# Ragged self-attention on one core: loops over pairs of ranks with doubled buffers, x transposed by the DMA crossbar, scores in batches of two

## The chip, the cores and the metric

The kernel runs on one core of a Trainium2 chip. TensorE (PE) multiplies, VectorE (DVE) and ScalarE (ACT) read its results out of PSUM, GpSimd (POOL) works from SBUF to SBUF, and SyncE (SP) issues DMAs on the core's 16 DMA engines. The metric is the device time of one execution in microseconds; less is better.

## The reference

Thirty-two sequences of up to 512 rows by 512 columns, each with its own length (75 to 502 in this draw; 64 to 511 by the rule), go through one projection and eight heads of softmax attention. Rows past the length are zero in the output.

```python
for b in range(batch):
    seq_len = lengths[b]
    qkv = np.matmul(x[b, :seq_len], w_qkv)
    q, k, v = np.split(qkv, 3, axis=-1)        # then 8 heads of 64 each
    ...
    scores = scale * np.matmul(q, k.transpose(0, 2, 1))
    attn = np.exp(scores - max)
    attn = attn / (np.sum(attn, axis=-1, keepdims=True) + 1e-08)
    output[b, :seq_len] = np.matmul(attn, v).transpose(1, 0, 2).reshape(seq_len, dim)
```

## The kernel before

**Ranks and classes.** The lengths are known only on the chip. DVE and one small PE matmul sort them, longest first; `idx` holds the order, `masks` the valid rows of each rank, and `ends` how many ranks are at least as long as each of 15 classes N = 512, 480, ... 64. Every engine loads the 15 ends into registers (`load_ends`) and walks the same While loops, one for each class (`loops`), with one rank as an iteration. T = ceil(N / 128) is the number of row tiles: in this draw 4 ranks have T = 4, 12 have T = 3, 11 have T = 2 and 5 have T = 1, and twelve classes are used; 480 and 416, between used ones, have no ranks and are jumped over.

**The pipeline.** The body of rank r computes the attention of rank r, and between its parts the projections of rank r + 1, so that PE has matmuls while ACT takes exponentials. The strings in `make_body` write out the order: S is one unit of scores (both heads of a head pair, one tile of keys) into one of two slots `psc`, evacuated by ACT's exponential into `ep` (L237); Q, K and V are projections into one of two banks `pa`, evacuated by DVE (L266, L299); A is the product with V into `pav`; M and X are the normalization of A on DVE: reciprocal (L357), mask (L364), multiplication into `onat` (L376). `v_aug` has a column of ones (mask values) for each head, so that A yields the softmax sum too.

**Buffers.** There is one `xT`, one `qkT`, one `v_aug`. At a body's end PE transposes the next rank's x16 through the banks `pa` (L397), ACT and DVE copy the results into `xT` (L402, L405), and the next body begins. Its first A takes both score slots free first (`acquire` of s0 and s1), and thus waits for the exponentials of the S just ahead of it.

**Other queues.** SP zero-fills rows past T tiles, loads x three ranks ahead when POOL has cast the one before (s_xfree), and stores the output in four pieces, one for a head pair (s_of, s_od). POOL casts x from float32 to float16. A PE wait shows in the profile as PEq at L35, the helper `take`; matmuls recorded as L424 are the first of a body.

Of the kernel before, what the change touches and what calls it, by code (L numbers as in the profile page):

```python
# [7 lines left out]
FP32 = mybir.dt.float32  # L8
F16 = mybir.dt.float16
I32 = mybir.dt.int32  # L10
# [7 lines left out]
NR = 36  # L18
# [3 lines left out]
class Prog:  # L22


    def __init__(self, busy):
        self.ops = {"pe": [], "act": [], "dve": []}
        self.busy = dict(busy)

# [44 lines left out]
def kernel(  # L73
# [25 lines left out]
    x_p = [sb("x_p0", [P, NT, D], FP32), sb("x_p1", [P, NT, D], FP32)]  # L99
# [8 lines left out]
    ident_f = sb("ident_f", [P, P], FP32)  # L108
    ident = sb("ident", [P, P], F16)
    len_b = sb("len_b", [P, 2 * B], I32)  # L110
    len_c = sb("len_c", [B, 2], I32)
    lenf = sb("lenf", [P, B], FP32)
# [6 lines left out]
    pos_i = sb("pos_i", [B, B], I32)  # L119
    pos_f = sb("pos_f", [B, B], FP32)  # L120
    rk_i = sb("rk_i", [B, NR], I32)
    rk_f = sb("rk_f", [B, NR], FP32)
    bi_i = sb("bi_i", [B, P], I32)
    bi_f = sb("bi_f", [B, P], FP32)
    thr_i = sb("thr_i", [1, len(CLASSES), B], I32)
    thr_f = sb("thr_f", [1, len(CLASSES), B], FP32)
# [5 lines left out]
    row_i = sb("row_i", [P, NT], I32)  # L132
    row_f = sb("row_f", [P, NT], FP32)
    masks = sb("masks", [P, NR - 2, 2, NT], FP32)
    rcp = sb("rcp", [P, NPAIR, 2 * NPAIR], FP32)
    junk = sb("junk", [P, 2], FP32)
# [4 lines left out]
    pa16 = pa.bitcast(F16)  # L141
# [4 lines left out]
    s_xp = [sem("s_xp0"), sem("s_xp1")]  # L146
    s_x = sem("s_x")
    s_const = sem("s_const")
    s_iota = sem("s_iota")
    s_r = sem("s_r")  # L150
    s_m = sem("s_m")
    s_self = sem("s_self")
    s_pself = sem("s_pself")
    s_hot = sem("s_hot")
    s_srt = sem("s_srt")
    s_tab = sem("s_tab")
    s_zero = sem("s_zero")
# [14 lines left out]
    free = {b: sem(f"e_{b}") for b in banks}  # L172

# [671 lines left out]
```

## Time and profile before

| | us |
|---|---|
| median of three runs | 527.71 (522.52 to 530.04) |
| the profiled execution | 529.94 |
| its span, first to last instruction | 528.1 |
| PE busy | 409.9 (78%) |
| PE's weight loads | 275.7 (52%) |
| DVE busy | 284.1 (54%) |
| ACT busy | 243.8 (46%) |
| POOL busy | 58.9 (11%) |
| mean granted PE clock | 0.94 |

A busy share is an average over some 58 us ahead of the loops, in which PE does little, and 32 bodies that get shorter and shorter. Weight loads overlap matmuls. The body's windows and the places where two bodies meet say more than the page's totals.

### The profile page before, as it was taken

How to read it: one execution, taken by the hardware profiler on the slowest of the kernel's cores; microseconds unless marked ns; L12 is line 12 of the kernel's file. 1: busy time of each engine (PE TensorE's matmuls, PEld its weight loads, DVE VectorE, ACT ScalarE, POOL GpSimd, SP SyncE). 2: the span in 40 equal slices, each digit the busy share in tenths (PEclk: the TensorE clock that was granted, in tenths of full speed). 3: DMA queues.
4: the chain of work that ended last, by engine and by line, in shares of the span. 5: the costliest groups of instructions: out<-in, count | busy, mean ns of one | idle time of the engine just before them, and what ended most of it. 6: DMA issues, size and time to landing. Idle time of an engine off the chain costs nothing. (4 is left out here: it accounts for less than half of the span.)

```text
span 528.1 us, 15112 instructions
## 1 busy us (share of the span) xinstructions
PE 409.9 (78%) x5090; PEld 275.7 (52%) x5090; DVE 284.1 (54%) x725; ACT 243.8 (46%) x299; POOL 58.9 (11%) x81
## 2 busy tenths in 40 slices
PE   0008895989895998898888988899888868886973
PEld 0013553555462555565555655665566656675752
DVE  8504552555452654565556555564465654665673
ACT  2003573767572664555556545454343343334331
POOL 9021101010101001101110011101000010001000
PEclk9999997999897998999999989998798898989899
DMA  4080221332313133233323333333333344544575
GB/s 161 1 318 0 80 60 35 113 92 85 123 40 103 50 120 126 68 103 124 124 70 109 124 114 106 101 104 124 119 122 122 128 137 141 166 154 139 169 247 204
DMA packets 60596, 61.07 MB, mean 116 GB/s; under 512 B 3088, under 2 KB 40976, under 8 KB 60560
## 3 DMA queue, kind: packets, MB, share of 16 engines
q1 hardware_dynamic: 59984, 58.50, 34.0%
q10 hardware_dynamic: 576, 2.10, 1.1%
q8 instruction: 21, 0.34, 0.3%
q14 instruction: 15, 0.12, 0.1%
HBM read 27.03 MB, written 33.55 MB: 115 GB/s over the span
## 5 line engine op out<-in xcount | busy, mean ns | idle before, releaser
L237 ACT ACTIVATE ep<-psc 128x896 f16<-128x896 f32 (+5 forms) x262 | 212.2, 810 | 189.5 <-ACTq L35 187.4
L197 PE MATMUL pa<-xT,w_r 128*128 128x352 f16 (+11 forms) x1050 | 168.5, 300 | 0.8 <-PEq L35 0.6
L266 DVE CAST qkT<-pa 128x352 f16<-128x352 f32 (+5 forms) x190 | 106.0, 558 | 88.4 <-DVEq L35 86.2
L197 PEld LDWEIGHTS pa<-xT,w_r 128*128 128x128 f16 x1050 | 83.0, 102 | 54.1 <-issue 29.8
L197 PE MATMUL pav<-v_aug,ep 128*128 128x65 f16 x1768 | 78.3, 199 | 38.0 <-PEq L35 37.8
L197 PE MATMUL pa<-w_r,xT 128*128 128x128 f16 (+1 forms) x1268 | 97.0, 227 | 0.1
L197 PEld LDWEIGHTS pav<-v_aug,ep 128*128 128x128 f16 x1768 | 67.4, 101 | 53.1 <-issue 50.4
L197 PE MATMUL psc<-qkT 64*128 64x352 f16 (+11 forms) x621 | 91.5, 311 | 1.5 <-PEq L35 1.5
L718 POOL CAST x<-x_nat 128x1536 f16<-128x1536 f32 (+3 forms) x32 | 39.8, 1242 | 436.1 <-POOLq L717 436.1
L197 PEld LDWEIGHTS pa<-w_r,xT 128*128 128x128 f16 x1268 | 80.1, 101 | 10.5 <-issue 5.3
L357 DVE RECIPROCAL rcp<-pav 128x6 f32<-128x6 f32 (+2 forms) x113 | 21.5, 190 | 94.4 <-DVEq L35 94.3
L402 ACT COPY xT<-pa 128x1024 f16<-128x1024 f16 (+2 forms) x34 | 29.7, 874 | 82.0 <-ACTq L35 82.0
L299 DVE TENSOR_TENSOR v_aug<-pa,masks 128x384 f16<-128x384 f32 (+2 forms) x112 | 59.4, 531 | 14.8 <-DVEq L35 13.0
L376 DVE TENSOR_TENSOR onat<-pav,rcp 128x384 f32<-128x384 f32 (+2 forms) x113 | 59.3, 525 | 7.3 <-DVEq L35 0.7
L397 PE MATMUL pa<-ident,x 128*128 128x128 f16 x348 | 28.4, 222 | 31.2 <-PEq L35 30.1
L197 PEld LDWEIGHTS psc<-qkT 64*128 64x128 f16 x621 | 26.8, 94 | 44.1 <-issue 32.3
L397 PEld LDWEIGHTS pa<-ident,x 128*128 128x128 f16 x348 | 21.2, 99 | 39.0 <-issue 39.0
L364 DVE TENSOR_SCALAR rcp<-rcp,masks 128x2 f32<-128x2 f32 (+1 forms) x113 | 25.2, 223 | 1.4 <-DVEq L35 1.0
L405 DVE COPY xT<-pa 128x768 f16<-128x768 f16 (+1 forms) x18 | 10.8, 602 | 24.5 <-DVEq L35 24.5
L424 PE MATMUL psc<-qkT 64*128 64x352 f16 (+9 forms) x27 | 8.0, 297 | 17.1 <-PEq L35 16.8
L727 PE MATMUL pav<-onehot,sel 32*128 32x36 f16 x2 | 0.2, 198 | 18.7 <-DVEq L69 18.7
L424 PEld LDWEIGHTS psc<-qkT 64*128 64x128 f16 x27 | 2.5, 93 | 20.9 <-issue 20.8
(50 smaller groups left out, 55.8 us busy)
## 6 DMA issues: line engine op xcount, KB each, us to landing
x_nat<-in_x_dram SPq DMA_DIRECT2D x12, 768.0 KB, 4.5
out_dram<-onat SPq DMA_DIRECT2D x48, 192.0 KB, 2.1
out_dram<-zt SPq DMA_DIRECT2D x11, 512.0 KB, 3.0
x_nat<-in_x_dram SPq DMA_DIRECT2D x11, 512.0 KB, 3.6
out_dram<-onat SPq DMA_DIRECT2D x44, 128.0 KB, 1.8
out_dram<-onat SPq DMA_DIRECT2D x21, 256.0 KB, 2.3
x_nat<-in_x_dram SPq DMA_DIRECT2D x5, 1024.0 KB, 5.4
out_dram<-zt SPq DMA_DIRECT2D x5, 768.0 KB, 3.7
```

The source lines that it names most:

```text
L197: return lambda e: e.matmul(o, lhsT, rhs, start=start, stop=stop)
L237: lambda e: e.activation(out=dst, in_=src, func=AF.Exp, scale=scale),
L266: group(pr, b, eng, mms, lambda e: e.tensor_copy(out=dst, in_=src))
L299: lambda e: e.tensor_tensor(out=v_aug[:, 0:T, 2 * i : 2 * i + 2, 0:HD], in0=pa[:, bank, 0 : T * P].rearrange("p (t a d) -> p t a d", a=2, ...
L357: lambda e: e.reciprocal(out=rv, in_=res[:, :, :, HD]).then_inc(s_r, 1),
L364: lambda e: e.tensor_scalar(out=last, in0=last, scalar1=3.0e38, scalar2=now[0][:, 1, T - 1 : T], op0=ALU.min, op1=ALU.mult,).then_inc(s_m, 1),
L376: lambda e: e.tensor_tensor(out=dst, in0=res[:, :, :, 0:HD], in1=rv.unsqueeze(3).broadcast_to([P, nq, 2, HD]), op=ALU.mult,).then_inc(s_of ...
L397: mms.append(lambda e, o=o, i_=i_: e.transpose(o, i_, ident))
L402: lambda e, d=dst, s=src: e.copy(out=d, in_=s))
L405: lambda e, d=dst, s=src: e.tensor_copy(out=d, in_=s))
L424: ins = f(*a, **k)
L718: e.tensor_copy(out=x16[:, 0:T, :], in_=x_nat[:, 0:T, :]).then_inc(s_x16, 1)
```

## The change

**Pairs.** A loop's iteration now holds two ranks, two halves h = 0 and 1, in the class of the first and longer one. `x_nat`, `x16`, `xT`, `qkT`, `v_aug` and `onat` exist twice, one for each half; half h computes the attention from buffers h and projects the next rank into buffers g = 1 - h. `ends` counts pairs.

**The crossbar.** SP issues one DMA transpose for each tile of 128 rows from `x16[h]` to `xT[h]` (`to_xT`), for the rank two ahead, at the start of half h when PE's first matmul there has said that `xT[h]` is free (s_xtf). PE waits for all of them (s_xt, 64) ahead of a half's first projection. PE's transposes, their copies on ACT and DVE and the identity matrix are gone.

**Batches.** `ORDER` writes S two at a time, and pair 0's scores of the next rank are the last of a half, not mixed with its own start. An A takes a score slot only if the slot last held scores of that head pair.

**Normalization.** For T = 2 and 3 two head pairs' A lie side by side in `pav`, and one reciprocal, mask and multiplication serve both. The output is stored in two pieces of 256 columns, not four of 128.

**POOL, SP and the start.** POOL also writes the ones of `v_aug`. x is loaded five ranks ahead. Ahead of the loops the iotas are written in float32, several DVE casts are gone, the V weights' cast goes from POOL to ACT, the memset of `ep` from POOL to DVE (with a new one of `qkT[1]`), and `load_ends` waits for s_end, after the sort, where `ends` used to be ready ahead of it.

On PE the names are the tiles: `psc` scores, `pa` projections (`xT,w_r` for Q and K, `w_r,xT` for V; `ident,x` transposes), `pav` products with V. Before, the end of the class of N = 384 and the start of N = 352:

```order
L397 MATMUL pa<-ident,x 128x128 x12
L584 REGISTER_ALU
L582 UNCONDITIONAL_BRANCH
L582 ISA
L582 COMPARE_AND_BRANCH
L424 MATMUL psc<-qkT 128x352
L197 MATMUL psc<-qkT 128x352
L197 MATMUL pav<-v_aug,ep 128x65 x18
L197 MATMUL psc<-qkT 128x352 x2
L197 MATMUL pa<-xT,w_r 128x352 x4
L197 MATMUL psc<-qkT 128x352 x2
```

PE at the same place now:

```order
L194 MATMUL pa<-xT,w_r 128x384 x4
L194 MATMUL pa<-w_r,xT 128x128 x12
L539 REGISTER_ALU
L537 UNCONDITIONAL_BRANCH
L537 ISA
L537 COMPARE_AND_BRANCH
L194 MATMUL psc<-qkT 128x352 x4
L194 MATMUL pa<-xT,w_r 128x352 x4
L194 MATMUL pav<-v_aug,ep 128x65 x18
L194 MATMUL pa<-xT,w_r 128x352 x4
L194 MATMUL psc<-qkT 128x352 x4
L194 MATMUL pa<-w_r,xT 128x128 x12
```

The twelve transposes are gone, scores stand four matmuls (two units) together, and a projection lies between them and the first product with V.

On SP one body of N = 352 before (`zt` is the zero fill, TENSOR_LOAD reads the rank's batch index):

```order
L631 DMA out_dram<-zt 128x512
L605 ISA
L606 TENSOR_LOAD idx
L607 ISA
L611 DMA x_nat<-in_x_dram 128x3x512
L605 ISA
L606 TENSOR_LOAD idx
L657 ISA
L657 DMA out_dram<-onat 128x3x128
L657 ISA
L657 DMA out_dram<-onat 128x3x128
```

SP in the first half of N = 352 now:

```order
L574 DMA_TRANSPOSE xT<-x_0 128x4x128 x2
L574 DMA_TRANSPOSE xT<-x_0 128x4x96
L546 ISA
L547 TENSOR_LOAD idx
L548 ISA
L610 DMA out_dram<-zt 128x512
L623 REGISTER_ALU
L623 DMA out_dram<-onat 128x3x256
L546 ISA
L547 TENSOR_LOAD idx
L548 ISA
L582 DMA x_nat<-in_x_dram 128x3x512
```

Three transposes stand ahead of the half's zero fill on the one queue, and the load comes behind the first output.

The diff, cut to its core:

```diff
-    x_nat = sb("x_nat", [P, NT, D], FP32)
-    x16 = sb("x16", [P, NT, D], F16)
-    xT = sb("xT", [P, NC, MAXS], F16)
-    qkT = sb("qkT", [P, 2 * NPAIR, MAXS], F16)
-    v_aug = sb("v_aug", [P, NT, NH, HD + 1], F16)
+    x_nat = [sb(f"x_nat_{h}", [P, NT, D], FP32) for h in range(2)]
+    x16 = [sb(f"x16_{h}", [P, NT, D], F16) for h in range(2)]
+    xT = [sb(f"xT_{h}", [P, NC, MAXS], F16) for h in range(2)]
+    qkT = [sb(f"qkT_{h}", [P, 2 * NPAIR, MAXS], F16) for h in range(2)]
+    v_aug = [sb(f"v_aug_{h}", [P, NT, NH, HD + 1], F16) for h in range(2)]
     ep = sb("ep", [P, NPAIR, 2, NT, MAXS], F16)
-    onat = sb("onat", [P, NT, D], FP32)
+    onat = [sb(f"onat_{h}", [P, 2, NT, 2 * P], FP32) for h in range(2)]
...
+        for b in ("s0", "s1"):
+            if pr.pair[b] == i or T == 1 and pr.pair[b] is not None:
+                acquire(pr, b)
...
+            jobs = [(256 * qt, i, qt) for qt in range(T)]
+        else:
+            jobs = [(74 * (4 * qt + 2 * (i % 2)), i, qt) for qt in range(T)]
...
+        if T in (2, 3) and i % 2 == 0:
+            acquire_carry(pr, mms)
+            return
...
-    def transposes(pr, T, engs, bank=0):
-        n = 2 if T >= 3 else 1
-        w = T * P
-        pr.take("pe", s_x16)
...
+    ORDER = {
+        4: "S S Q0 A0 S S K0 V0 S S Q1 A1 S S K1 V1 S S Q2 A2 S S K2 V2 S S Q3 A3 S S K3 V3",
+        3: "S S Q0 A0 K0 S S V0 Q1 A1 S S K1 V1 S S Q2 A2 K2 S S V2 Q3 A3 S S K3 V3",
+        2: "S S B0 w A0 V0 B1 A1 V1 S S B2 w A2 V2 B3 A3 V3",
+    }
+
+    def half(pr, h, T, N, st):
+
+        g = 1 - h
+        pr.signals += [s_xtf[h], s_vf[g]]
+
+        def start_proj():
+            if not st["x"]:
+                st["x"] = True
+                pr.take("pe", s_xt[g], 64)
+                pr.signals.append(s_x16f[g])
...
+        units = [(i, k) for i in (1, 2, 3, 0) for k in range(per)]
+        first = True
+        for tok in ORDER[T].split():
+            if tok == "S":
+                i, k = units.pop(0)
+                scores(pr, st["slot"], g if i == 0 else h, i, k, T, N)
+                st["slot"] ^= 1
+            elif tok == "w":
+                acquire(pr, "a1")
+            elif tok[0] == "A":
+                if first:
+                    first = False
+                    pr.take("pe", s_on[h])
+                attnv(pr, h, int(tok[1]), T)
...
-                        0: "S A S Q M S K X S V",
...
-            transposes(pr, T, ["act", "dve"])
...
+        for h in range(2):
+            st["x"] = False
+            pr.add("dve", lambda e: set_now(e))
+            half(pr, h, T, N, st)
+            pr.add("dve", lambda e: e.reg_add(rank_reg[0], rank_reg[0], 1))
...
+        pr.take("pe", s_xt[0], 64)
+        pr.signals.append(s_x16f[0])
...
+            def to_xT(h, N):
+                T = -(-N // P)
+                for t in range(T):
+                    n = min(P, N - t * P)
+                    e.dma_start_transpose(
+                        out=xT[h][:, :, t * P : t * P + n], in_=x16[h][0:n, t, :]
+                    ).then_inc(s_xt[h], 16)
+                if T < NT:
+                    e.nop().then_inc(s_xt[h], 16 * (NT - T))
...
+                for h in range(2):
+                    wait_dec(e, s_xtf[h])
+                    to_xT(h, N)
+                    bi = batch_of(e, rank, tmp, 0)
+                    if T < NT:
                         e.dma_start(
+                            out=out[bass.ds(bi, 1), T * P : MAXS, :].rearrange(
+                                "o (t p) d -> p (o t) d", p=P
+                            ),
+                            in_=zt.unsqueeze(1).broadcast_to([P, NT - T, D]),
+                        ).then_inc(s_zd, 16)
+                    else:
+                        e.nop().then_inc(s_zd, 16)
+                    for j in range(2):
+                        if T > 1 or j == 0:
+                            wait_dec(e, s_of[h][j])
+                        if j == 1:
+                            bi = batch_of(e, rank, tmp, 0)
+                        e.dma_start(
+                            out=out[
+                                bass.ds(bi, 1), 0 : T * P, 2 * j * P : 2 * (j + 1) * P
+                            ].rearrange("o (t p) d -> p (o t) d", p=P),
+                            in_=onat[h][:, j, 0:T, :],
+                        ).then_inc(s_od[h][j], 16)
+                        if j == 0:
+                            wait_dec(e, s_xc[1 - h])
+                            load(1 - h, 5, T)
+                    e.reg_add(rank, rank, 1)
...
+            e.wait_ge(s_wv, 16)
+            e.copy(
+                out=w_r[:, :, 2 * D : 3 * D], in_=w_f[:, :, 2 * D : 3 * D]
+            ).then_inc(s_wr["v"], 1)
...
+                    wait_dec(e, s_vf[1 - h])
+                    rv = e.snap(rank, min_val=0, max_val=B - 1)
+                    ones(1 - h, T, masks[:, bass.ds(rv, 1), :, :].rearrange(
+                        "p o a t -> p (o a) t"))
+                    wait_dec(e, s_x16f[1 - h])
+                    cast(1 - h, T)
+                    e.reg_add(rank, rank, 1)
...
+            e.memset(ep[:, 1:NPAIR], 1.0)
+            e.memset(qkT[1], 0.0)
```

## Rows read from the trace of the kernel before

**Rows 1.** The page, parts 1 and 2, the whole span.

```profile
PE 409.9 (78%) x5090; PEld 275.7 (52%) x5090; DVE 284.1 (54%) x725; ACT 243.8 (46%) x299; POOL 58.9 (11%) x81
...
PEclk9999997999897998999999989998798898989899
```

**Rows 2.** Windows of one body: length, busy times, granted clock, DMA share, GB/s.

```profile
111.85:135.07 23.22, 21.11 (x272) 12.63 (x273) 12.41 (x26) 15.69 (x17) 1.92 (x2) 1.00 0.30 90
...
220.25:238.57 18.32, 16.53 (x188) 10.32 (x189) 10.18 (x27) 9.88 (x14) 1.49 (x2) 0.91 0.31 100
...
255.43:272.32 16.89, 15.11 (x189) 9.71 (x190) 10.19 (x27) 9.89 (x14) 1.49 (x2) 1.00 0.35 109
...
423.24:434.29 11.05, 8.27 (x120) 6.85 (x121) 6.83 (x22) 4.93 (x6) 1.07 (x2) 1.00 0.44 142
...
465.92:476.59 10.67, 8.62 (x120) 7.12 (x121) 6.07 (x22) 3.73 (x6) 1.07 (x2) 0.84 0.48 147
...
476.59:486.06 9.47, 7.32 (x120) 6.02 (x121) 5.98 (x22) 3.73 (x6) 1.07 (x2) 1.00 0.51 166
...
511.70:516.93 5.23, 3.46 (x56) 2.42 (x57) 3.10 (x8) 1.30 (x3) 0.64 (x2) 1.00 0.88 310
```

**Rows 3.** Timeline of PE, N = 352: start, length, operation, idle before it.

```profile
269.90 0.83 PE L197 MATMUL pa<-w_r,xT 128*128 128x128 f16 x12
...
270.89 0.49 PE L397 MATMUL pa<-ident,x 128*128 128x128 f16 x6 [0.15 <-PEq L35]
...
272.32 0.31 PE L424 MATMUL psc<-qkT 64*128 64x352 f16 x1 [0.23 <-PEq L35]
...
273.83 0.34 PE L197 MATMUL pav<-v_aug,ep 128*128 128x65 f16 x6 [1.19 <-PEq L35]
```

**Rows 4.** Timeline of PE where bodies meet, N = 448, 224 and 96.

```profile
132.19 1.07 PE L197 MATMUL pa<-w_r,xT 128*128 128x128 f16 x16
...
135.07 0.35 PE L424 MATMUL psc<-qkT 64*128 64x448 f16 x1
...
136.79 0.43 PE L197 MATMUL pav<-v_aug,ep 128*128 128x65 f16 x5 [1.35 <-PEq L35]
...
421.56 0.61 PE L197 MATMUL pa<-w_r,xT 128*128 128x128 f16 x8
...
423.24 0.25 PE L424 MATMUL psc<-qkT 64*128 64x224 f16 x1 [0.23 <-PEq L35]
...
425.39 0.40 PE L197 MATMUL pav<-v_aug,ep 128*128 128x65 f16 x8 [1.79 <-PEq L35]
...
507.14 0.20 PE L424 MATMUL pa<-xT,w_r 128*128 128x96 f16 x1 [0.66 <-PEq L35]
```

**Rows 5.** Timeline of PE where the class 480 is skipped.

```profile
86.98 0.53 PE L424 MATMUL psc<-qkT 64*128 64x448 f16 x1 [4.47 <-PEq L35]
```

**Rows 6.** Timeline of all engines ahead of the loops.

```profile
3.10 10.96 DVE L62 CAST bi_f<-bi_i 32x128 f32<-32x128 int32 x1
...
15.67 0.18 DVE L62 CAST lenf<-len_b 128x32 f32<-128x32 int32 x1
...
26.21 0.42 SPq L611 DMA_DIRECT2D x_p<-in_x_dram  x1
...
36.24 1.90 POOL L709 CAST x<-x_p 128x2048 f16<-128x2048 f32 x1
...
41.29 0.59 PE L424 MATMUL pa<-xT,w_r 128*128 128x512 f16 x1 [1.14 <-PEq L35]
```

**Rows 7.** Chain that ended last, its last piece.

```profile
521.62 0.82 ACT ep L237
```

**Rows 8.** DMA: the SP queue, and two issues with median us to landing.

```profile
q1 hardware_dynamic: 59984, 58.50, 34.0%
...
out_dram<-onat SPq DMA_DIRECT2D x44, 128.0 KB, 1.8
...
len_c<-in_lengths_dram SPq DMA_DIRECT2D x1, 0.2 KB, 6.1
```

More of the change, by code (lines that the diff above doesn't have):

```diff
@@ L172 @@
     free = {b: sem(f"e_{b}") for b in banks}
+    now = [None]
     def acquire(pr, b):
@@ new lines @@
+    CANON = {b: True for b in banks}
+    ORDER = {
[3 rows of a table added]
+    }
[7 more added lines that the diff above has]
+                pr.signals.append(s_x16f[g])
+        if T == 1:
+            start_proj()
+            qk(pr, st["bank"], g, [(i, 0) for i in range(NPAIR)], N, P)
+            qk(pr, st["bank"] ^ 1, g, [(i, 1) for i in range(NPAIR)], N, P)
+            pr.take("pe", s_on[h])
+            attnv(pr, h, 0, 1)
+            vproj(pr, st["bank"], g, 0, 1)
+            acquire(pr, f"a{st['bank'] ^ 1}")
+            scores(pr, h, g, 0, 0, 1, N)
+            st["bank"] ^= 1
+            return
+        per = T if T >= 3 else 1
+        units = [(i, k) for i in (1, 2, 3, 0) for k in range(per)]
[10 more added lines that the diff above has]
+                    first = False
+                    pr.take("pe", s_on[h])
+                attnv(pr, h, int(tok[1]), T)
+            else:
+                start_proj()
+                i = int(tok[1])
+                if tok[0] == "V":
+                    vproj(pr, st["bank"], g, i, T)
+                elif tok[0] == "B":
+                    qk(pr, st["bank"], g, [(i, 0), (i, 1)], N, 256)
+                else:
+                    qk(pr, st["bank"], g, [(i, "QK".index(tok[0]))], N, MAXS)
+                st["bank"] ^= 1
+        assert not units
@@ L525, in make_body, with set_now @@
                 pr.add("pe", lambda e, b=b: e.sem_inc(free[b], 1))
-        first_mm_frees_x16(pr)
+        assert not pr.signals
         return pr
+    rank_reg = [None]
+    def set_now(e):
+        rv = e.snap(rank_reg[0], min_val=0, max_val=B - 1)
+        now[0] = masks[:, bass.ds(rv, 1), :, :].rearrange("p o a t -> p (o a) t")
     def make_bridge():
-        pr = Prog(CANON)
-        acquire(pr, "s0")
-        acquire(pr, "s1")
-        scores(pr, 0, 0, 0, 1, P)
-        pr.add("pe", lambda e: e.sem_inc(free["s1"], 1))
+        pr = Prog(CANON, 0)
+        for b in banks:
+            acquire(pr, b)
+        scores(pr, 1, 0, 0, 0, 1, P)
+        for b in banks:
+            if not pr.busy[b]:
+                pr.add("pe", lambda e, b=b: e.sem_inc(free[b], 1))
         return pr
@@ L546, in make_prologue @@
         for i in range(NPAIR):
[L547 to L548 removed]
+            for f in range(2):
+                qk(pr, bank, 0, [(i, f)], MAXS, MAXS)
                 bank ^= 1
@@ L573, in load_ends @@
             regs.append(g)
-        r = e.alloc_register("rank")
+        r = e.alloc_register("pair")
         e.reg_mov(r, 0)
@@ L661, in _ @@
             loops(e, regs, r, body)
-            for k in range(NPAIR):
-                e.wait_ge(s_od[k], 16)
+            for h in range(2):
+                for j in range(2):
+                    e.wait_ge(s_od[h][j], 16)
             e.wait_ge(s_zd, 16 * B)
@@ L733, in _ @@
             prologue.run("pe", e)
-            loops(e, regs, r, lambda e, N, r: bodies[N].run("pe", e),
+            loops(e, regs, r, lambda e, N: bodies[N].run("pe", e),
                   lambda e: bridge.run("pe", e))
@@ L800, in _ @@
             regs, r = load_ends(e)
-            now[0] = masks[:, NR - 3, :, :]
+            rank_reg[0] = e.alloc_register("rank")
+            e.reg_mov(rank_reg[0], 0)
+            now[0] = masks[:, B, :, :]
             prologue.run("dve", e)
-            def body(e, N, r):
-                rv = e.snap(r, min_val=0, max_val=NR - 4)
-                now[0] = masks[:, bass.ds(rv, 1), :, :].rearrange("p o a t -> p (o a) t")
-                bodies[N].run("dve", e)
-            loops(e, regs, r, body)
+            loops(e, regs, r, lambda e, N: bodies[N].run("dve", e))
 _INS = ['x', 'w_qkv', 'lengths', 'n_heads']
```

552 lines of the change are left out of this document (207 added, 345 removed), and 7 rows, old and new, of the table seq.

## The prediction

> **What bounds the kernel now.** I read the page's busy shares first, then windows of single bodies, then PE's timeline where one body ends and the next begins, and the stretch ahead of the loops.
>
> PE is the busiest engine, 409.9 us of a span of 528.1, and its clock is granted in full except in dips [rows 1]. A body of three tiles (N = 352) takes 16.89 us, with PE busy for 15.11, DVE for 10.19, ACT for 9.89 and the DMA engines for 0.35 of it [rows 2]. So PE sets the pace inside a body, and the question is what stands between one body's useful matmuls and the next one's.
>
> At N = 352 the last V projection ends at 269.90 + 0.83 = 270.73, and the next body's first score matmul starts at 272.32: 1.59 us for the transposes of x and their copies. PE then waits another 1.19 us before the first product with V, because it needs the exponentials of scores that it has only just issued [rows 3]. Together 2.78 us per body. With four tiles it is 133.26 to 135.07 and 1.35, so 3.16; with two tiles 422.17 to 423.24 and 1.79, so 2.86; with one tile a wait of 0.66 and some 0.3 of transposes, 1.0 [rows 4].
>
> The clock is a second price of the same gap. Two bodies of the same N = 352 take 18.32 us at a granted clock of 0.91 and 16.89 at 1.00, and two of N = 160 take 10.67 at 0.84 and 9.47 at 1.00 [rows 2]. Fifteen of the 31 bodies after the first have a window at 0.94 or less, the first and the last of that kind in rows 2 being 0.91 and 0.84. The stretch before each cold one is a gap as above.
>
> Ahead of the loops, DVE loses 10.96 us in one small cast, the lengths are used from 15.67, x is fetched from 26.21, cast at 36.24 after the V weights, and PE's first projection starts at 41.29 [rows 6]. The loops begin at 58.01.
>
> **The change part by part.** I sum from the profiled execution: 58.0 us ahead of the loops, 464.4 us of loops (the last exponential ends at 521.62 + 0.82 = 522.4 [rows 7]), 5.7 to the end of the span, and 1.8 between the span and the execution's 529.94 us. The median of the runs, 527.71, lies 0.4% below that execution.
>
> *Transposes and the wait at a body's start go.* PE issues no transposes, ACT and DVE copy no xT. In the new order a half begins with scores for pair 1 and a projection, and pair 0's exponentials date from the half before, so the 1.2 to 1.8 us wait has its cover: two scores, Q0, and the projections that ended the half before. Gain: 4 ranks x 3.16 + 12 x 2.78 + 11 x 2.86 + 5 x 1.0 = 82.5 us.
>
> *The clock.* With these gaps gone, the dips after them should go. Fifteen cold bodies, eight of three or four tiles at 18.32 - 16.89 = 1.43 and seven of two tiles at 1.20, are 20 us. Two stretches of about 4.5 us remain where a class of no ranks is skipped, one of which is shown [rows 5]; their bodies stay cold, so I take 17.
>
> *Rounding by pairs.* The second rank of a pair is computed at the first one's N. Six steps of 32 columns are added (from 11.05 at N = 224 to 9.47 at N = 160 is 0.8 a step with a class change in the longer one; I take 0.7), and the rank of 119 goes from one tile to two: 9.47 - 2.86 less 3.6, so 3. Cost: 7 us.
>
> *One normalization per two head pairs.* For two and three tiles 92 groups of three DVE operations become 48. DVE is busy for 10.19 of 16.89 us [rows 2], and PE after this change still needs 16.89 - 2.78 = 14.1. It is hidden either way: nothing.
>
> *Batches of two scores.* Each pair of scores must find both slots free. ACT was busy for 9.89 us in 14 operations, so some 0.75 for an exponential of N = 352 [rows 2]; two and their hand-overs, 1.5 + 0.4, fit in the 2.1 us of the shortest PE stretch between batches (K, V and the two scores). That is tight. I take 0.5 us of new waiting per half, 32 x 0.5 = 16 us; the bounds are 0 and the 1.2 us of today's wait, 38.
>
> *Ahead of the loops.* The lengths land at about 1.4 + 6.1 = 7.5 us [rows 8]. The sort then has five short DVE operations before its matmul, where there were nine after 15.67; the class ends are now formed after the order, so I set x's fetch at about 17 (before, 10.5 us passed from 15.67 to 26.21; 9.5 are kept). From the fetch to the first projection before took 15.1 us [rows 6], with the V weights' cast of 1.9 in it, which goes to ACT; the PE transposes and copies, some 3 us, become four crossbar transfers at 4 to 6. DVE's two added memsets run beside the loads. First projection at about 30.5, loops from 46. Gain: 12, between 8 and 14.
>
> *The crossbar transfers* are what the trace does not show. Each moves 128 x 512 halves, 128 KB; a half issues T of them on SP, behind the half before's output and ahead of its own zero fill, output and load. They have about one half to land before PE asks (its wait on s_xt ahead of Q0). From below: 58.50 MB took 34.0% of the engines' span, 326 GB/s while busy, so 128 KB is 0.40 us. In pieces of 128 halves it is 512 packets; 59,984 packets in that time are 48 ns each on one engine, so 512 on 16 engines are 1.5 us. If each waits for the one before, a store of 128 KB lands in 1.8 us and is issued in 0.4: 2.2 us [rows 8]. I take 1.0, between the first two, since a packet's price includes packets four times as large. Then a half of two tiles has 0.51 x 9.47 = 4.8 us of other traffic plus 2.0, against 6.6 of PE at N = 160; three tiles 5.9 + 3.0 against 14.1; four 7.0 + 4.0 against 20; one tile up to 0.88 x 5.23 = 4.6 plus 1.0 against some 4 [rows 2]. Hidden but for the four short ranks, at about 1 us each: 4 us.
>
> The Trainium skill (VectorE: DVE Perf Modes, The three transpose paths) speaks against this part: it gives 1309 ns for a 128 x 128 transpose by the crossbar, 390 by TensorE, and advises TensorE where a result in PSUM will do. What hangs on it stands in the third rival. The skill's page DMA: Bandwidth & Descriptors (Latency and other measured facts) gives 261 GB/s for such transfers, an estimate of 0.5 us for 128 KB, by which the 4 us above would vanish. No run before shows either.
>
> **Sum.** Ahead 46; loops 464.4 - 82.5 - 17 + 7 + 16 + 4 = 391.9; end 5.7: span 443.6. With 1.8 outside and less the 0.4%, **444 us**.
>
> **The rivals.** *The crossbar paces the short ranks.* At 2.2 us each, one after another, a half of two tiles needs 4.8 + 4.4 = 9.2 us of DMA against about 7.1 of PE, twelve times, and one of one tile 6.8 against 4, four times; three and four tiles stay covered (5.9 + 6.6 under 14.1). That adds some 25 + 11 to the sum without its last 4: 476. For it: one queue, in order, and DMA already at 0.5 in these bodies. Against: 16 engines can hold several transfers.
>
> *The batches hand a wait back.* If two exponentials and their hand-overs do not fit, PE waits at each batch: some 130 batches x 0.5 more over the 16 already taken is 50 us: about 493. Against: ACT is at 46% and loses its copies.
>
> *Slower: the crossbar becomes the bound.* If a transfer is worked as four blocks of 128 columns, each landing before the next (4 x 1.8 = 7.2 us), a half takes its plain traffic plus T times that: 4 x 35.8 + 12 x 27.5 + 12 x 19.2 + 4 x 11.8 = 751 us of loops, some 820 in all. The place is PE's wait on s_xt ahead of Q0. It decides from 3.7 us a transfer: 4 x 21.8 + 12 x 17.0 + 12 x 12.2 + 4 x 8.3 = 471 of loops, plus 46, 16 for skipped and changed classes, and 7.5, 540. Against: 326 GB/s on the same engines.
>
> By the skill's 1309 ns, four blocks are an estimate of 5.2 us, past that point, and some 660 us.
>
> *The gaps only move.* If PE, freed of transposes, waits in the same place for DVE or for code at the loop's head, the gain stays near the 12 us ahead of the loops: 515. Code for two halves is twice as long, but today's return to a loop's head costs PE at most 0.2 us [rows 3, 4].
>
> **How the numbers follow.** Chances: forecast 0.58, paced by the crossbar 0.20, batches 0.08, gaps that move 0.04, bound by the crossbar 0.10. The likeliest gives 444. The range goes from 420 (no new waits, transfers at 0.4) to 510, which takes in the first two rivals and new waits at their bound; what lies outside is the slower case and the gaps that move. A measurement of this kernel can tell about 2% (517 to 538) from no change. Faster 0.87, within 2% 0.03, slower 0.10.
>
> **What would show it.** Right: windows of N = 352 halves of 14 to 15 us with PE busy nearly throughout at clock 1.00; no PE idle ahead of the first product with V; the first projection near 30 us; transposes landing within a half. Wrong: PE idle ahead of the first projection of a half with SP or a DMA as its releaser (crossbar), or ahead of scores in each batch (ACT), a clock that still dips, or a loop head with several us of idle.

## The result, and the profile after

| | before | after |
|---|---|---|
| median, us | 525.95 (522.52 to 530.04, 4 runs) | 438.26 (436.65 to 439.65, 4 runs) |
| the profiled execution | 529.94 | 437.63 |
| its span | 528.1 | 435.8 |

The ratio is 0.8329, with an interval of [0.8256, 0.8402]: 444 was forecast, within 420 to 510. The same kernel measured again beside three of the experiments gave 435.56 us and 0.8282 [0.8217, 0.8347], so a difference of 2 us between kernels that were not measured side by side means nothing.

The page of the kernel after, parts 1 and 2, answers to [rows 1]:

```profile
PE 352.6 (81%) x4802; PEld 251.6 (58%) x4802; DVE 258.4 (59%) x536; ACT 209.3 (48%) x269; POOL 56.5 (13%) x81
...
PEclk9999999989998999999999999999999998999885
```

PE is busy for 57 us less, and the clock dips in three slices and in the last three, where twelve did. The windows of one half at N = 352 and of one at N = 224 (length, busy PE, PEld, DVE, ACT, POOL, granted clock, DMA share, GB/s) answer to [rows 2]:

```profile
186.99:200.33 13.34, 12.98 (x176) 8.84 (x176) 8.74 (x19) 8.59 (x13) 1.76 (x2) 1.00 0.53 165
...
329.46:337.87 8.41, 7.71 (x113) 6.29 (x114) 5.68 (x13) 3.45 (x4) 1.29 (x2) 1.00 0.59 181
```

A rank of three tiles takes 13.34 us where it took 16.89, one of N = 224 takes 8.41 where it took 11.05. Both of the latter are the shortest of their class: before, the three took 11.72, 11.73 and 11.05, and now the four took 9.76, 10.22, 8.41 and 9.12. By row tiles, the windows of the loops' stretches show where the gain lies:

| | before, us | after, us |
|---|---|---|
| four tiles | 106.13, 4 ranks | 83.64, 4 ranks |
| three | 210.24, 12 | 160.91, 12 |
| two | 123.68, 11 | 112.16, 12 |
| one | 24.38, 5 | 23.22, 4 |

Three and four tiles gain 71.8 us, two tiles 11.5.

The timeline of PE (start, length, operation, idle before it and its releaser) where two halves of N = 352 meet, and in halves of two tiles and of one, answers to [rows 3, 4]; two more lines show its longest kinds of idle, to compare with [rows 5]:

```profile
89.13 0.93 PE L194 MATMUL psc<-qkT 64*128 64x448 f16 x4 [3.38 <-PEq L37]
...
186.52 0.47 PE L194 MATMUL psc<-qkT 64*128 64x352 f16 x4
186.99 0.76 PE L194 MATMUL pa<-xT,w_r 128*128 128x352 f16 x4
187.59 0.72 PE L194 MATMUL pav<-v_aug,ep 128*128 128x65 f16 x18
188.14 0.76 PE L194 MATMUL pa<-xT,w_r 128*128 128x352 f16 x4
188.83 0.47 PE L194 MATMUL psc<-qkT 64*128 64x352 f16 x4
189.24 0.84 PE L194 MATMUL pa<-w_r,xT 128*128 128x128 f16 x12
...
193.76 0.76 PE L194 MATMUL pa<-xT,w_r 128*128 128x352 f16 x4 [0.28 <-PEq L37]
...
321.77 0.65 PE L194 MATMUL pa<-xT,w_r 128*128 128x224 f16 x5 [1.58 <-issue]
...
339.98 0.40 PE L194 MATMUL pav<-v_aug,ep 128*128 128x65 f16 x8 [0.68 <-PEq L37]
...
416.50 2.52 PE L194 MATMUL pa<-xT,w_r 128*128 128x96 f16 x32 [4.08 <-PEq L37]
```

At three tiles the scores, Q and the first product with V (187.59) follow without a pause, where 1.19 us of wait stood; a batch in the middle of the half is followed by 0.28. At two tiles the pause ahead of A0 and A2 is still there, 0.68 here: this is the token w. An empty class still costs 3.38. New are idles named "issue", in the middle of a group of matmuls, five in halves of two tiles.

The start (all engines) answers to [rows 6], DVE's last operation, which ends the chain now, with SP's last issues around it to [rows 7]:

```profile
14.56 10.30 DVE L774 MEMSET ep<- 128x12288 f16 x1 [2.83 <-issue]
...
15.26 1.50 SPq L582 DMA_DIRECT2D x_nat<-in_x_dram  x2
...
22.89 5.24 SPq L574 DMA_TRANSPOSE xT<-x  x4
...
29.64 3.57 PE L194 MATMUL pa<-xT,w_r 128*128 128x512 f16 x8 [22.00 <-PEq L37]
...
425.11 1.84 SPq L574 DMA_TRANSPOSE xT<-x  x1
425.86 0.74 DVE L279 TENSOR_SCALAR v_aug<-pa,masks 128x512 f16<-128x512 f32 x1
...
429.91 0.36 SPq L582 DMA_DIRECT2D x_nat<-in_x_dram  x1
430.88 0.34 SPq L623 DMA_DIRECT2D out_dram<-onat  x1
```

The loops begin at 46.68 and end with DVE at 426.60; the last output is issued at 430.88, behind a transpose and a load that nobody reads any more. The DMA view (issue: count, median us to landing) answers to [rows 8]:

```profile
xT<-x SPq DMA_TRANSPOSE x88, 2.5
```

A crossbar transpose of 128 x 512 halves landed 2.5 us after its issue (the median), and four of them kept SP for 5.24 us, 1.3 each, one after the other. All the transfers of this queue together come to 71.00 MB, where they were 58.50.

### The profile page after: what moved, and what is told of

Its sections match the earlier page's. It is cut to its first block, busy times and chain, and to the rows that moved or that the text cites. A ratio compares the mean times of both kernels' runs of the same rounds, so it can differ in the third digit from the quotient of the medians.

```text
span 435.8 us, 13753 instructions
## 1 busy us (share of the span) xinstructions
PE 352.6 (81%) x4802; PEld 251.6 (58%) x4802; DVE 258.4 (59%) x536; ACT 209.3 (48%) x269; POOL 56.5 (13%) x81
## 5 line engine op out<-in xcount | busy, mean ns | idle before, releaser
L236 ACT ACTIVATE ep<-psc 128x704 f16<-128x704 f32 (+5 forms) x265 | 204.0, 820 | 193.7 <-ACTq L37 193.7
L194 PE MATMUL pa<-xT,w_r 128*128 128x352 f16 (+11 forms) x1056 | 167.1, 296 | 37.7 <-PEq L37 34.7
L194 PE MATMUL psc<-qkT 64*128 64x352 f16 (+11 forms) x656 | 70.8, 302 | 12.6 <-PEq L37 11.2
L387 DVE TENSOR_TENSOR onat<-pav,rcp 128x512 f32<-128x512 f32 (+1 forms) x68 | 53.4, 785 | 10.4 <-DVEq L37 0.5
L687 POOL CAST v_aug<-masks 128x24 f16 (+4 forms) x33 | 9.0, 274 | 331.0 <-POOLq L543 331.0
L682 POOL CAST x<-x_nat 128x1536 f16<-128x1536 f32 (+3 forms) x35 | 45.8, 1308 | 34.9 <-POOLq L543 34.4
L194 PEld LDWEIGHTS psc<-qkT 64*128 64x128 f16 x656 | 25.7, 93 | 36.1 <-issue 25.1
L361 DVE RECIPROCAL rcp<-pav 128x8 f32<-128x8 f32 (+1 forms) x68 | 14.4, 212 | 6.1 <-DVEq L37 5.4
L367 DVE TENSOR_SCALAR rcp<-rcp,masks 128x4 f32<-128x4 f32 (+2 forms) x36 | 8.3, 230 | 7.3 <-DVEq L37 7.3
L774 DVE MEMSET ep<- 128x12288 f16 x1 | 10.3, 10298 | 2.8 <-issue 2.8
L376 DVE SCALAR_TENSOR_TENSOR rcp<-rcp,masks 128x8 f32<-128x8 f32 (+1 forms) x32 | 5.4, 169 | 6.0 <-DVEq L37 3.4
```

What stands on the lines that cost most here:

```text
L194: return lambda e: e.matmul(o, lhsT, rhs, start=start, stop=stop)
L236: lambda e: e.activation(out=dst, in_=src, func=AF.Exp, scale=scale),
L361: lambda e: e.reciprocal(out=rv, in_=den).then_inc(s_r, 1),
L367: lambda e: e.tensor_scalar(out=last, in0=last, scalar1=3.0e38, scalar2=now[0][:, 1, T - 1 : T], op0=ALU.min, op1=ALU.mult,).then_inc(s_m, 1),
L376: lambda e: e.scalar_tensor_tensor(out=byt, in0=byt, scalar=3.0e38, in1=now[0][:, 1, 0:T].unsqueeze(2).broadcast_to(list(byt.shape)), op0= ...
L387: ins = e.tensor_tensor(out=dst, in0=num, in1=rv.unsqueeze(len(sh) + 1).broadcast_to([P, *sh, HD]), op=ALU.mult,)
```

## The experiments

All start from the kernel after, but for the three that build on another experiment (memsets on POOL and early fetch; no w and early start; the last adding 13 classes to that). Ratios are to the kernel before, measured beside each.

| run | us, median of 4 | ratio, 95% interval |
|---|---|---|
| transposes back on PE | 478.79 | 0.9122 [0.908, 0.9163] |
| single units of scores | 471.50 | 0.9002 [0.8959, 0.9045] |
| each crossbar transpose twice | 463.82 | 0.8851 [0.8821, 0.888] |
| normalization per head pair, T = 2, 3 | 440.52 | 0.8398 [0.8358, 0.8438] |
| the same at T = 2 alone, no w | 430.76 | 0.8184 [0.8139, 0.8229] |
| no zero fills | 432.59 | 0.8185 [0.8125, 0.8245] |
| memsets on POOL | 448.60 | 0.8518 [0.8468, 0.8568] |
| memsets on POOL, early fetch | 441.05 | 0.8365 [0.8314, 0.8416] |
| 13 classes | 419.84 | 0.7981 [0.7916, 0.8046] |
| no w, early start | 426.13 | 0.8112 [0.8045, 0.818] |
| no w, early start, 13 classes | 411.98 | 0.7847 [0.7782, 0.7912] |
| the kernel after, again | 435.56 | 0.8282 [0.8217, 0.8347] |

### Transposes back on PE

```diff
+        transposes(pr, h, T, st["bank"])
...
-                    e.dma_start_transpose(
-                        out=xT[h][:, :, t * P : t * P + n], in_=x16[h][0:n, t, :]
```

> The changed kernel with the crossbar alone undone: PE transposes x16 through the banks of the projections at the start of each half, ACT and DVE copy one bank each, an identity matrix is made by POOL, SP issues no DMA transposes; pairs, batches and the joint normalization stay. Theory (PE sets the pace, and the transposes were PE's and its wait): the part of the old gap that was transposes and copies comes back, 1.81 us at four tiles, 1.59 at three, 1.07 at two, 0.3 at one, that is 4 x 1.81 + 12 x 1.59 + 11 x 1.07 + 5 x 0.3 = 40 us, less where the batch of scores covers the copies: 465 to 480, likeliest 474. Rival (the crossbar only trades PE's time for SP's and the DMA engines' time, and the gain of 88 us came from pairs, order and start): 430 to 447.

478.79 us, a ratio 0.079 to 0.084 above the kernel after: 42 to 44 us, the theory's size. A half of N = 352 shows where, by its window and by PE's timeline at its start:

```profile
189.76:204.63 14.87, 13.86 (x188) 9.46 (x189) 9.29 (x20) 9.16 (x13) 1.76 (x2) 1.00 0.37 126
```

```profile
189.76 0.96 PE L413 MATMUL pa<-ident,x 128*128 128x128 f16 x12 [0.67 <-PEq L37]
```

It takes 14.87 us against 13.34: 0.88 more of busy PE, and a wait of 0.67 for a bank that DVE still empties. Over the whole class of N = 352 (six halves, first scores to first scores) it is 89.62 against 80.20, 1.57 a half, where the prediction read 1.59 from [rows 3]. The crossbar's gain is PE's time. The rival falls.

The Trainium skill (VectorE: DVE Perf Modes, The three transpose paths) gives 390 ns a block by TensorE against 1309 by the crossbar, and the same page (Rules for kernel authors) advises TensorE where a result in PSUM will do. The trace disagrees on the price: four blocks landed in 2.5 us, which the page's figure would make 5.2 (an estimate). On the advice it disagrees as well: what counted here was whose time it is, not how long it takes.

### Single units of scores

```diff
-        3: "S S Q0 A0 K0 S S V0 Q1 A1 S S K1 V1 S S Q2 A2 K2 S S V2 Q3 A3 S S K3 V3",
-        2: "S S B0 w A0 V0 B1 A1 V1 S S B2 w A2 V2 B3 A3 V3",
+        3: "S Q0 S A0 K0 S V0 S Q1 S A1 K1 S V1 S Q2 S A2 K2 S V2 S Q3 S A3 K3 S V3",
+        2: "S B0 w A0 S V0 B1 A1 V1 S B2 w A2 S V2 B3 A3 V3",
```

> The changed kernel with the batches alone undone: the same units of scores, but one at a time, each with a projection or a product with V between. The prediction's theory (batches of two make PE wait for ACT, 16 us): faster, about 422 to 432. Theory from the trace after (the four matmuls of a batch follow each other in 0.40 us, the two of a single unit took 0.51 for two units' worth twice, about 0.1 us more for two units, some 130 pairs of units, and PE's waits at the batches are 0.2 to 0.3 us, few): slower by some 5 to 15, about 448. Third: no difference, 434 to 442.

471.50 us: the prediction's sign was wrong, and the theory's size (5 to 15 us) less than half of what was measured, 35 to 38 us by the ratios. Its groups of matmuls by line and tile (busy us, mean ns, idle before them and releasers), its window of one half of N = 352, and its PE there:

```profile
L194 PE MATMUL pa<-xT,w_r 128*128 128x352 f16 (+11 forms) x1056 | 165.1, 293 | 41.6 <-PEq L37 40.7 <-issue 0.8
...
L194 PE MATMUL psc<-qkT 64*128 64x352 f16 (+11 forms) x656 | 91.2, 305 | 13.8 <-PEq L37 12.7 <-issue 1.0
L194 PE MATMUL pav<-v_aug,ep 128*128 128x65 f16 x1792 | 75.9, 196 | 18.4 <-PEq L37 18.4
```

```profile
186.78:201.99 15.21, 14.13 (x177) 8.56 (x178) 8.81 (x19) 9.04 (x13) 1.70 (x2) 1.00 0.49 145
```

```profile
172.96 0.76 PE L194 MATMUL pa<-xT,w_r 128*128 128x352 f16 x4
173.65 0.32 PE L194 MATMUL psc<-qkT 64*128 64x352 f16 x2
173.91 0.84 PE L194 MATMUL pa<-w_r,xT 128*128 128x128 f16 x12
...
179.17 0.76 PE L194 MATMUL pa<-xT,w_r 128*128 128x352 f16 x4 [0.66 <-PEq L37]
```

The same groups of the kernel after:

```profile
L194 PE MATMUL pa<-xT,w_r 128*128 128x352 f16 (+11 forms) x1056 | 167.1, 296 | 37.7 <-PEq L37 34.7 <-issue 2.5
L194 PE MATMUL pa<-w_r,xT 128*128 128x128 f16 (+1 forms) x1296 | 96.0, 223 | 3.3 <-issue 3.2
L194 PE MATMUL pav<-v_aug,ep 128*128 128x65 f16 x1792 | 75.0, 195 | 11.2 <-PEq L37 11.0
L194 PE MATMUL psc<-qkT 64*128 64x352 f16 (+11 forms) x656 | 70.8, 302 | 12.6 <-PEq L37 11.2 <-issue 1.3
```

Two causes, both in these rows. PE's busy time for scores is 91.2 against 70.8, 20 of the 23 us by which PE as a whole is busier (375.5 against 352.6). A single unit takes 0.26 us from its start to the next group's (173.65 to 173.91), so two take 0.52, and a batch of two takes 0.41 (188.83 to 189.24 in the kernel after). Entering the scores costs as well: a projection of four matmuls lasts 0.69 from start to start ahead of scores (172.96 to 173.65, and 188.14 to 188.83) and 0.60 ahead of a product with V (186.99 to 187.59). So each batch in place of two single units saves some 0.2 us of PE, six times a half: 1.15 by the windows (14.13 less 12.98). The second cause: waits at L37 grew by 15 us in these groups, among them the one ahead of Q (0.66 at 179.17, against 0.28): one unit of scores covers less than two of DVE's normalization and of the evacuation of K that stands behind it. That the scores' other shape (64 rows of the array where the projections use 128) is why entering them costs was not tested. By tiles, the single units add 9.6 us at four, 21.2 at three and 6.0 at two.

### Each crossbar transpose twice

```diff
-                    e.dma_start_transpose(
-                        out=xT[h][:, :, t * P : t * P + n], in_=x16[h][0:n, t, :]
-                    ).then_inc(s_xt[h], 16)
+                    for dst in (xS, xT):
+                        e.dma_start_transpose(
+                            out=dst[h][:, :, t * P : t * P + n], in_=x16[h][0:n, t, :]
+                        ).then_inc(s_xt[h], 16)
```

> The changed kernel with every crossbar transpose issued twice, the first copy into a spare buffer that nobody reads; PE waits for both. SP's issues took 1.25 us each in the trace after. Theory (hidden for two tiles and more): ahead of the loops four more issues stand before the first projection, +5; the halves of one tile each wait for one more issue, +1.3 x 4; the rest nothing: 446 to 452. Rival (the crossbar is already near its limit in halves of two tiles): each of those waits 2 to 2.5 us more, 12 x 2.5 = 30 on top, 475 or more. Rival of the prediction's slower case (bound by it everywhere): 84 transposes x 2.5 = 210 us more.

463.82 us, between theory and rival. The first projection starts 5.2 us later, as the theory had it. At three and four tiles no wait for a transpose appears (N = 352: 80.25 us for the class against 80.20). But at two tiles some halves wait, by PE's timeline and SP's (the last of the issues):

```profile
370.31 0.82 PE L195 MATMUL pa<-xT,w_r 128*128 128x192 f16 x8 [2.98 <-PEq L37]
```

```profile
366.67 2.22 SPq L576 DMA_TRANSPOSE xT<-x  x1
```

The last issue begins at 366.67 and PE goes on at 370.31, so the wait is the last transpose's landing. Six halves of two tiles wait 1.1 to 3.2 us, and those of one tile 1.5 to 4.3. Of the 25.4 us between the two spans, 11.9 lie at two tiles and 7.6 at one; the loops begin 3.0 later, and 3.2 at three and four tiles are mostly longer idles ahead of a class and dips of the clock. So the crossbar is hidden at two tiles as it stands, but in half of those halves its margin is below the 2.5 us that two more issues take.

### One normalization for each head pair

```diff
-            jobs = [(74 * (4 * qt + 2 * (i % 2)), i, qt) for qt in range(T)]
+            jobs = [(MAXS * (i % 2) + 130 * qt, i, qt) for qt in range(T)]
...
-        if T in (2, 3) and i % 2 == 0:
-            acquire_carry(pr, mms)
-            return
```

> The changed kernel with the joint normalization alone undone for two and three tiles: reciprocal, mask and multiplication for each head pair, in their own halves of pav. The prediction's theory (hidden under PE, costed at nothing): 436 to 440. Rival (DVE's shorter chain is what lets PE run on, above all at two tiles, where PE waits for DVE ahead of two of the four products with V): about 0.3 us in each of 24 halves of two and three tiles or more, 445 to 455. Third (the wait at two tiles is made by the joint normalization, which is longer in one piece, so that undoing it shortens the wait): 430 to 436.

440.52 us; its interval overlaps that of the kernel after. By class, from first scores to first scores, it loses at three tiles (N = 352: 82.30 against 80.20; all four classes together 3.5 us) and is even at two (192 and 160 shorter by 0.9 and 0.8, 256 and 224 longer by 0.5 and 0.8 than in the second measurement). So the joint normalization is worth some 3.5 us at three tiles, and at two it can't be told from nothing: the half of N = 192 that ran at a lower clock in the kernel after, which cost it some 1.7 us (next section), ran at 1.00 here.

### The same at two tiles alone, without w

```diff
-        if T in (2, 3) and i % 2 == 0:
+        if T == 3 and i % 2 == 0:
...
-        2: "S S B0 w A0 V0 B1 A1 V1 S S B2 w A2 V2 B3 A3 V3",
+        2: "S S B0 A0 V0 B1 A1 V1 S S B2 A2 V2 B3 A3 V3",
```

> The changed kernel with one normalization per head pair at two tiles alone, in two halves of pav, and so without the token w (the wait for bank a1 ahead of A0 and A2). In the trace after, 18 such waits took 11.0 us; A0 waits there for the joint normalization and for the V evacuation that stands behind it on DVE. Theory (the joint normalization, which the prediction costed at nothing, is paid at two tiles by this wait): 427 to 433. Rival (DVE is busy for 6.25 of 8.14 us of a half of N = 224, and two more chains of three operations make it late for the next projection's bank instead): 436 to 441.

430.76 us, 5 to 8 less by the ratios. Its groups say that this is not the theory's gain alone:

```profile
L194 PE MATMUL pa<-xT,w_r 128*128 128x352 f16 (+11 forms) x1056 | 162.7, 289 | 38.9 <-PEq L37 37.3 <-issue 0.7
L194 PE MATMUL pa<-w_r,xT 128*128 128x128 f16 (+1 forms) x1296 | 95.5, 222 | 7.6 <-PEq L37 7.0
L194 PE MATMUL pav<-v_aug,ep 128*128 128x65 f16 x1792 | 75.0, 195 | 0.0
L194 PE MATMUL psc<-qkT 64*128 64x352 f16 (+11 forms) x656 | 70.6, 301 | 12.9 <-PEq L37 11.8 <-issue 1.0
```

The 11.0 us ahead of `pav` are gone, but 7.0 stand now ahead of V's projection and 2.6 more ahead of Q and K: the rival's late DVE takes most of it back. The rest comes from two places that the edit was not aimed at. The idles named "issue" were 7.0 us in the kernel after (2.5 + 3.2 + 1.3 in its groups) and are 1.7 here (0.7 + 1.0). And two halves ran at a lower clock in the kernel after, the second of N = 192, which has waits of 0.78 and 1.53 us in it, and the first of one tile:

```profile
354.89:366.63 11.74, 8.60 (x114) 7.38 (x113) 6.15 (x18) 3.02 (x4) 1.29 (x2) 0.85 0.68 197
...
403.39:408.19 4.80, 4.80 (x52) 4.04 (x53) 1.66 (x4) 0.49 (x1) 0.83 (x2) 0.67 0.75 261
```

Without w the same two halves ran at 1.00:

```profile
355.59:364.31 8.72, 7.34 (x115) 6.17 (x113) 6.67 (x23) 3.02 (x4) 1.29 (x2) 1.00 0.70 209
...
397.55:400.88 3.33, 3.33 (x53) 2.56 (x53) 1.66 (x4) 0.58 (x1) 0.83 (x2) 1.00 0.67 214
```

In the kernel after, the half of N = 192 just ahead has 6.92 us of busy PE, so the lower clock cost the second some 1.7, and the one of one tile 1.5. The edit changed the code's length, and the idles may have moved with it. That their cause is instruction fetch was only argued: in the kernel after, each of the five begins 0.7 to 1.3 us behind the start of a transfer on the queue of instructions, but of the 35 packets there (21 in the kernel before) most have no such idle behind them.

### Without the zero fills

```diff
-                    if T < NT:
-                        e.dma_start(
-                            out=out[bass.ds(bi, 1), T * P : MAXS, :].rearrange(
...
+                    e.nop().then_inc(s_zd, 16)
```

> The changed kernel without the zero fills of the rows past T tiles (those rows of the output are left unwritten): 13.8 MB of 71 less on the one DMA queue, 28 issues of 0.4 us less on SP. Theory (the backlog of the queue makes the transposes of the halves of one tile late, one wait of 4.08 us, and the end 3.5 us longer than before): 429 to 434. Rival (the transposes are late there because SP issues them behind the output of the half before, which it does all the same): 436 to 439.

432.59 us, with runs from 428.45 to 434.69: some gain, of unsettled size. But PE's waits at one tile are no shorter:

```profile
415.08 1.52 PE L194 MATMUL pa<-xT,w_r 128*128 128x96 f16 x32 [2.84 <-PEq L37]
420.46 2.57 PE L194 MATMUL pa<-xT,w_r 128*128 128x96 f16 x32 [2.39 <-PEq L37]
```

Together 5.2 us, against 4.08 and 0.89. On SP the transpose waited for at 415.08 is issued at 412.33, behind the output of the half before at 411.79, as in the kernel after (412.04 behind 411.49). So the rival explains those waits, and the zero fills cost at the end: from DVE's last operation to the span's end it is 6.7 us here and 9.2 in the kernel after. Another 2.4 us are gone at two tiles (109.74 against 112.16), where the half of N = 192 ran at 1.00.

### The memsets on POOL, and the early fetch

```diff
             e.memset(zt, 0.0).then_inc(s_zero, 1)
+            e.memset(ep[:, 1:NPAIR], 1.0)
+            e.memset(qkT[1], 0.0).then_inc(s_ms, 1)
```

> The changed kernel with the memsets of ep and qkT[1] back on POOL, at its start, beside DVE's sort; ACT waits for them ahead of its first exponential. In the trace after, the memset of ep took 10.30 us on DVE, and DVE's share of the weights was cast at 26.92 to 28.15, with the first projection at 29.64. Theory (before, DVE's 10.96 us in one small cast was POOL's memset beside it, on the SBUF port that the two share): the sort and so the fetch of x come some 5 to 8 us later, 443 to 447. Rival (the cast was long for another reason): the fetch stays at 15.3, the first projection at 29 to 30, limited by the transposes: 436 to 439.

448.60 us: the theory's mechanism, at more than its size, for the first projection starts at 39.50 where it was 29.64. DVE's first cast and POOL's memsets, by the timeline:

```profile
5.96 10.49 DVE L737 CAST sel<-len_c 32x128 f16<-32x128 int32 x1 [5.96 <-DMA len_c<-in_lengths_dram]
```

```profile
2.59 10.33 POOL L695 MEMSET ep<- 128x12288 f16 x1
12.87 3.50 POOL L696 MEMSET qkT<- 128x4096 f16 x1
```

A cast that took 0.21 us in the kernel after took 10.49 and ended at 16.45, with POOL's second memset at 16.37; the cast of 10.96 in [rows 6] stood beside POOL's memset of `ep` (3.65 to 13.99 in that trace) in the same way. The Trainium skill (SBUF — State Buffer, Who interferes with whom) has it so: DVE's casts can need the port pair that it shares with GpSimd, and the later one waits for the whole instruction. The trace agrees, but DVE waited through two instructions of POOL.

The next kernel adds, on SP, the register loads moved from the head of the queue to behind the fetch of the V weights:

```diff
-            regs, r = load_ends(e)
...
+            e.wait_ge(s_srt, 1)
...
             ).then_inc(s_wv, 16)
+            regs, r = load_ends(e)
```

> As the kernel with the memsets on POOL, and SP issues the first two fetches of x and the V weights as soon as the order is known, ahead of its 15 register loads of the class ends (the order was known at 8.0 us in the trace after, x fetched at 15.26). Theory (the start's chain is order, fetch, cast, transposes): if the sort is not delayed by POOL, fetch near 9.5, first projection near 24, 432 to 434; if it is delayed by 5 to 8, 438 to 441. Rival (the weights or the V columns are what the start waits for): 437 to 440 with the fetch early.

441.05 us, 7.5 below the kernel before it, measured beside it, with the sort delayed as there: the fetch moved from 25.33 to 19.07 and the first projection from 39.50 to 33.19. The order, the fetch, the cast and the transposes are the start's chain, and 15 register loads stood in it.

### Thirteen classes

```diff
-CLASSES = [32 * k for k in range(16, 1, -1)]
+CLASSES = [512, 448] + [32 * k for k in range(12, 1, -1)]
```

> The changed kernel with 13 classes in place of 15: 480 and 416, which have no ranks in this draw, are left out of the list, so that no engine jumps over a loop between used classes at four tiles (lengths of 449 to 480 would be computed at 512, those of 385 to 416 at 448; here there are none at such a place). In the trace after, PE waited 3.38 us ahead of the first scores of 448 and 3.13 ahead of those of 384. Theory (the wait is the jump over a loop's code): some 6 us less, 430 to 433. Rival (it is the price of coming to a new loop after a class, and stays): 436 to 440.

419.84 us against 435.56 for the kernel after beside it: 15.7 less, the theory's sign at more than twice its size. Windows of the first half of N = 448 and of N = 384 in the kernel after, measured again:

```profile
87.51:107.32 19.81, 19.81 (x257) 12.96 (x258) 11.26 (x23) 13.80 (x16) 2.22 (x2) 0.91 0.39 106
...
128.70:143.84 15.14, 14.95 (x177) 9.55 (x178) 8.12 (x17) 8.96 (x12) 1.75 (x2) 0.89 0.43 124
```

The same halves with 13 classes:

```profile
83.53:101.76 18.23, 18.23 (x258) 12.27 (x256) 12.10 (x25) 13.86 (x17) 2.23 (x2) 1.00 0.51 143
...
119.99:133.93 13.94, 13.46 (x178) 8.85 (x176) 8.81 (x17) 8.95 (x12) 1.74 (x2) 1.00 0.59 172
```

The two idles were 3.64 and 3.09 in that execution and are gone; behind each the clock had been granted at 0.91 and 0.89 where it is now 1.00, another 1.58 and 1.20. That makes 9.5. Classes 224, 192 and 160 are shorter by 1.9, 2.4 and 2.7: of 7.0 us of "issue" idles 2.2 are left, and the half of N = 192 that took 11.61 us at a granted clock of 0.85 takes 9.39 at 1.00. The code behind the removed loops lies elsewhere now; that this is why those idles went was not shown.

### A version that beats both

On top of the kernel without w: SP's early fetch, DVE's weights ahead of its memset, and `ep` set to one by ACT.

```diff
+            e.activation(
+                out=epf,
+                in_=zt.unsqueeze(1).broadcast_to([P, epf.shape[1], D]),
+                func=AF.Exp,
+            )
```

> The kernel without w (one normalization per head pair at two tiles), and a shorter start: SP fetches x as soon as the order is known, ahead of its register loads; DVE casts its weights ahead of the memset of qkT[1]; ep is set to one by ACT (an exponential of the zero tile), idle at that time, so that neither POOL nor DVE is held. Theory (the two gains add: 7.5 from w, and the chain of order, fetch, cast, transposes 5 to 6 shorter, first projection near 24 us): 423 to 427. Rival (the start then waits for the V weights or for ACT's setting of ep, some 13 us from 9 on): 428 to 431.

426.13 us, 9.4 below the kernel after beside it. The start, all engines:

```profile
8.85 10.44 ACT L664 ACTIVATE ep<-zt 128x12288 f16<-128x12288 f32 x1
9.02 1.51 SPq L592 DMA_DIRECT2D x_nat<-in_x_dram  x2
...
23.14 3.55 PE L194 MATMUL pa<-xT,w_r 128*128 128x512 f16 x8 [15.48 <-PEq L37]
```

The first projection is 6.4 us earlier; the other gain shrank to 3. Two tiles kept theirs (106.93 us, and 107.13 without w alone), but against the kernel after beside it one tile lost 2.0 (23.45 us to PE's last matmul, and 21.42), and N = 384 lost 1.1.

> The two kernels before in one: no w, early start, 13 classes. If all three gains are of different stretches, they add: 417 to 421. If the class change keeps its price, 423 to 427.

411.98 us, 23.6 below the kernel after: 15.7 and 9.4, less 1.5. The list of classes fits this draw of lengths; the 426.13 of the run before doesn't depend on it.

> The changed kernel as it is, beside the three others on the same chip, as their measure: 436 to 440 by every theory.

435.56 us.

## Why the prediction was right, step by step

*What bounds the kernel: right.* PE's time in the body and the gaps between bodies were the price. Where transposes return to PE, all of their 1.57 us a half comes back.

*Transposes and the first wait: right at three and four tiles, half right at two.* The first A no longer waits at N = 352. At two tiles the wait for exponentials became one for the normalization, through w: 11.0 us in 18 waits.

*The clock: right, but for three more cold halves.* 3 us were left for two cold bodies; the windows above show 1.58 and 1.20. Three halves were cold besides, which the forecast did not have: the second of N = 192 and the first of one tile (1.7 and 1.5 us), and the first of N = 96, granted 0.68 behind the wait of 4.08, with 4.51 us of busy PE where the next half has 2.99.

*Joint normalization at nothing: near in its sum, wrong in its reason.* DVE is not simply hidden: the order of its work decides when `pav` and the banks come free. It gains 3.5 us at three tiles, and at two it makes the 11.0 us of w, of which no more than some 1.4 were to be had (11.0 less 7.0 and 2.6), because DVE is late either way.

*Batches of two scores at +16 us: wrong in sign*, and the largest error. PE's time falls by 23 us against single units; the wait that follows a batch is 0.2 to 0.3 at N = 352, and 0.67 at most at three tiles, and what is waited for is DVE, not ACT. The prediction weighed ACT alone and took PE's 14.1 us a half as given. The half came out at 13.34, below the 14 to 15 that it named as its sign.

*Crossbar transfers at 1.0 us: mis-sized.* They land in 2.5, a little above the largest of the three bounds, and are issued at 1.25 apiece. The first rival's price was thus the true one, and yet its 476 did not come. It added the transfers to the other traffic of a half; the doubled run shows that they fit at two tiles with less than 2.5 us to spare. At one tile the 4 us forecast are 5.6 (0.65 + 4.08 + 0.89).

*Ahead of the loops: right*, 46.7 against 46 (44.8 in the second measurement), with the fetch at 15.26 where 17 was set. *The end: 9.2 against 5.7.* The last output stands behind a transpose and a load for ranks that don't exist.

*Rounding by pairs (7 us)* was not tried apart, and neither were the pairs and the doubled buffers: no experiment takes them back.

The loops took 379.9 us and not 391.9. From 391.9, less 16 for waits that did not come and 23 of PE's time, plus 11.0 for w, 7.0 of "issue", 7 of waits for banks of projections (34.7 less 22.0 of the start and 5.6 at one tile), 1.6 at one tile, and less 2.5 for shorter jumps over empty classes, it is 377; some 3 us are left over, of the order of what the three cold halves took. By tiles the two errors stand apart. The prediction's own terms make a gain of some 45 us at three and four tiles and some 25 at two (an estimate: the gaps and the clock, less the batches, the rounding and the rank that moves to two tiles); the loops gained 71.8 and 11.5. So the median came out near 444 in part by luck: two unforeseen costs, w and "issue", paid back half of the unforeseen gain from the batches.

The second rival (batches hand a wait back) fell with the single units. The third fell with the landing of 2.5 us, below the 3.7 from which it decides. That gaps move was true only of two tiles.

## What to carry to other kernels

A transfer that takes longer than the engine's own way can still win, if the engine that sets the pace is rid of it and half a loop covers it; double the transfer to learn its margin. Here the scores' matmuls were cheaper two units together than scattered, and the mean of one did not show it (305 ns and 302): read from start to start. A loop that is jumped over is not free: here each of two cost over 3 us of idle and a half at a lower clock behind it.

## What the runs showed of the hardware

- Four crossbar transposes of 128 x 512 halves keep SP for 5.24 us, and one lands in 2.5 (the median of the 88 in the kernel).
- Scores of 64 x 352 take 0.26 us a unit alone, and a batch of two saves some 0.2 us of PE, part of it in the group ahead.
- DVE's cast of 0.21 us took 10.49 while POOL set 32 KB a partition in two memsets (10.33 and 3.50 us); ACT sets the same `ep` in 10.44 us, DVE in 10.30, and beside either POOL's cast of x took its 1.9 us.
- An empty loop between two used ones: 3.1 to 3.6 us of idle PE, then a half at a granted clock of 0.89 to 0.91 (a mean between the levels of 1.2 and 2.4 GHz).
